# A hybrid layer on one core: the weight sums of a group one slot apart and moved by three or four slots, and each sum stored by itself

## The chip, the cores and the metric

One core of a Trainium2 chip. Its engines are TensorE (PE, matmuls), VectorE (DVE), ScalarE (ACT), GpSimd (POOL) and SyncE (SP). DMA transfers are issued from SP and from ACT. The metric is the device time of one execution in microseconds (us); a kernel's time is the median of its runs.

## The reference

One layer of a streaming encoder, on 256 frames of width 4096, in fp32. One input projection feeds two groups of heads and a gate; a second projection and a LayerNorm close the layer:

```python
proj = einsum('bsd,dc->bsc', x, w_in)
# fox q|k|v|f, rwkv r|k|v|w_down|a_down, gate z
fox_out = fox_attention(q, k, v, log_sigmoid(f + f_bias))   # 16 heads of 128
rwkv_out = groupnorm(rwkv7_scan(r, decay, k, v, -kk, kk * a)) + bonus   # 32 heads of 64, chunks of 64 frames
h = concat([fox_out, rwkv_out]) * silu(z)
out = einsum('bsc,cd->bsd', h, w_out)
x = layernorm(ALPHA * x + out, ln_gain, ln_bias)
```

## The kernel before

**The input projection.** It is cut into 8 groups (n = 0 to 7) of 4 blocks (b = 0 to 3); a block is 512 columns. The 4096 rows of the weights make 32 k tiles of 128. fp32 operands are split in two: a rounded high part and the rest, so each product takes three matmuls per half of the frames (lines 162, 163 and 164: low frames by high weights and so on; line 164 is the one that needs the low part of the weights). Per pair q of k tiles there is one load of 512 KB from SP's queue (line 266, tile `w`), one cast to the high part on ACT (line 156, tile `w_qh`, 4 buffers) and one subtract for the low part on DVE (line 157, tile `w_ql`, 3 buffers). So w_12 is the pair q = 12, k tiles 24 and 25. In the text, w_12 or w_13 without a block number is that of block 1.

**The slots.** After each k tile the loop over a block calls `slot()`, which advances every piece of side work (a generator) by one `yield`. A group has 4 x 32 = 128 slots. Engines run their instructions in the order in which they were issued here, as far as the scheduler leaves it, so a slot is a place in each engine's queue, not a time. The side work of a steady group is:

- `prepare` with `front`: the decays and keys of a head pair. SP loads `raw` (line 330) and the low-rank weights `upt` (line 470); ACT makes `uph` (475), `tw` (487), `ta` (489), `eL` (496) and `eI` (498), both from `L`, which DVE scans (493); then `am` (501), and DVE `ae` (503) from `eI`; then `k` (541), `sb` (544), `hq` and `hr` (510, 512), `lc` (550), `lt` (551, 552) and `BK` (557).
- `rwkv`: the recurrence over four chunks, with matmuls `rh`, `up` and `sp`, whose results ACT and DVE copy to `R` (706), `UV` (737) and `SV` (748); then `yp`, and its norm (`post`, `hqy`, `hry`).
- `gate`: products `h` and their split `hl` (433 to 437), stored to DRAM as `hd` by SP (330). `fox`: attention, with `nb` loaded by SP (796, 797) and `fo` (826). `unload`: the copy `bk` of a finished block out of PSUM by ACT (1125), its transposes and its way through DRAM.
- `weight_sums` (lines 839 to 869), which the change touches.

**The weight sums.** Two pairs of blocks of the output projection use, for eight pairs q of k tiles, differences of four 128x512 blocks of `w_o`. They are made long before, during the input projection: 16 sets, two in each group. A set is four loads of 256 KB into the tile `ts` (128x4x512, one buffer), four subtracts on DVE (line 864, in place) and the stores to a scratch tensor `td` in DRAM, from which the output projection loads them after 1674 us. Loads and stores are issued from ACT's queue, both by `send`, line 847, in program order. `SETS` (line 55) gives for each of a group's two sets the slot at which its loads begin and how many slots later the subtracts may begin. `until` waits for a slot, `wait(n)` lets n slots go by. Since `ts` has one buffer, the loads of a set wait until the stores of the last one have read it.

**The output projection** follows the last group, then the LayerNorm. The change doesn't touch them.

Of the kernel before, what the change touches and what calls it, by code (L numbers as in the profile page):

```python
# [51 lines left out]
TAIL = 3  # L52
STARTS = (3, 5)
RING = (4, 3)
SETS = ((0, 12), (30, 8))
W = {"fo": 7, "vs": 2, "np": 4, "gp": 5, "tp": 4, "d1": 8, "d2": 12, "xp": 3, "fs": 4, "fp": 5}
NB = D // OB

# [37 lines left out]
def layer(ctx: ExitStack, tc: tile.TileContext, xt, xtok, w_main, w_lora, w_first, muv, w_o, up, par, mulora, fbias, lng, lnb, cst, out):  # L96
# [76 lines left out]
    for n, (k0, k1) in enumerate(pieces):  # L173
        for k in range(k0, k1):
            t = xpool.tile([P, 2, S], F32R, tag=f"x{k}", name=f"x{k}")
# [33 lines left out]
    def wait(n):  # L209
        for _ in range(n):  # L210
            yield
# [25 lines left out]
    tds = {(b, q): dram.tile([P, 4, OB], F32, name=f"td{b}_{q}") for b in STARTS for q in FEW}  # L237
# [607 lines left out]
    def weight_sums():  # L845
        def send(out, src):
            tc.keep_in_program_order(nc.scalar.dma_start(out=out, in_=src))

        def until(at):
            while where[0] < at:  # L850
                yield

        per = KT * 4
        places = [(n * per + (0 if n else KT) + o, gap) for n in range(G // 2) for o, gap in SETS]
        for (b, q), (at, gap) in zip(tds, places, strict=True):
            yield from until(at)
            t = rp.tile([P, 4, OB], F32, tag="ts", name=f"ts{b}_{q}")
            for n in range(4):
                send(t[:, n], w_o[b + n // 2][:, 2 * q + n % 2, :])
                yield  # L860
            yield from until(at + gap)
            b11, b21, b12, b22 = (t[:, n] for n in range(4))
            for o, x, y in ((b11, b12, b11), (b12, b22, b12), (b22, b22, b11), (b21, b21, b22)):
                nc.vector.tensor_tensor(o, x, y, ALU.subtract)
                yield from wait(2)
            yield from wait(3)
            for n in (2, 0):
                send(tds[b, q][:, n : n + 2], t[:, n : n + 2])
                yield from wait(2)

    def chain():
        for n in range(G // 2):
# [236 lines left out]
    side(gates())  # L1109
    side(chain())  # L1110
    side(weight_sums())
    vt = None
    for n in range(G // 2):
# [84 lines left out]
    for kind, b, q in plan:  # L1198
# [3 lines left out]
        if pair:  # L1202
            n = count[pair] = count[pair] + 1
# [245 lines left out]
```

## Time and profile before

| | |
|---|---|
| runs | 1912.09 us median of 3 (1911.28 to 1915.17) |
| profiled execution | 1909.98 us, of which the span 1908.2 |
| PE busy | 1897.1 us, 99% |
| DVE busy | 1477.3 us, 77% |
| ACT busy | 1010.5 us, 53% |
| POOL busy | 248.9 us, 13% |
| DMA | 466.75 MB, mean 245 GB/s |
| TensorE clock granted | 0.999 |

The span is the time of the core's work; the execution's own time has 1.8 us around it. In the rows of a timeline the columns are the start in us, the duration in us, the engine, the line, the operation, the output and the inputs; in brackets stands the idle time of the engine just before, and what ended it. "ACTq" and "SPq" are the queues from which DMAs are issued. In a row of the waits, the numbers are the total in us, the number of waits and the longest. In a row of the windows each engine has its busy time and, in brackets, its instructions, in the order PE, weight load, DVE, ACT, POOL; then come the granted clock, the DMA engines' share and GB/s.

### The profile page before, as it was taken

To read this page: it belongs to the slowest core of one execution; us is meant where nothing else is said; L and a number is where in the kernel's file an instruction comes from. 1 tells how busy PE (TensorE), PEld (TensorE's weight loads), DVE (VectorE), ACT (ScalarE), POOL (GpSimd) and SP (SyncE) were. 2 spreads that over 40 slices of the span, in tenths; PEclk is the share of its full clock that TensorE was granted. 3 is DMA by queue.
4 is the path that set the end of the run, shared out by engine and by line. 5 is a ranking of instruction groups with operands and counts; after the bars stand their busy time and mean duration, and the time that the engine had idled before them with its cause. 6 is when DMAs were issued, how large, how long until landed. Compare 5 with 4: busy or idle time off the path is not lost.

```text
span 1908.2 us, 28381 instructions
## 1 busy us (share of the span) xinstructions
PE 1897.1 (99%) x9745; PEld 1573.9 (82%) x9745; DVE 1477.3 (77%) x2521; ACT 1010.5 (53%) x1575; POOL 248.9 (13%) x467
## 2 busy tenths in 40 slices
PE   9999999999999999999999999999999999999998
PEld 9887888888888888888888888888888878888885
DVE  7688878787778777868787887687878775887876
ACT  6554455455545554555456544654465554455552
POOL 0022002211121122112111220122012200000000
PEclk9999999999999999999999999999999999999999
DMA  9688778887788787878787788778877975878883
GB/s 348 204 259 246 220 238 258 234 236 224 249 243 241 225 256 230 247 220 259 227 246 225 252 236 246 221 249 234 249 222 245 299 264 181 275 257 300 301 289 128
DMA packets 288262, 466.75 MB, mean 245 GB/s; under 512 B 144435, under 2 KB 171717, under 8 KB 288117
## 3 DMA queue, kind: packets, MB, share of 16 engines
q1 hardware_dynamic: 274004, 431.03, 73.7%
q10 hardware_dynamic: 14112, 33.90, 4.7%
q8 instruction: 76, 1.25, 0.3%
q14 instruction: 70, 0.57, 0.1%
HBM read 418.43 MB, written 46.42 MB: 244 GB/s over the span
## 4 chain that ended last, share of the span: by engine, by line
PE 96%; DVE 2%; DMA 1%; ACT 1%; issue 0%; SPq 0%; DVEq 0%; ACTq 0%
PE acc L162 24%; PE acc L164 24%; PE acc L163 23%; PE oacc L991 5%; PE oacc L992 5%; PE oacc L994 5%; PE gp L589 1%; PE rh L703 1%; PE p L991 1%; PE p L994 1%; PE p L992 1%; PE up L734 1%; PE sp L744 1%; PE accl L162 1%; PE accl L164 1%; PE accl L163 1%
## 5 line engine op out<-in xcount | busy, mean ns | idle before, releaser
L818 POOL COPY pT<-lg 32x96 f32<-32x96 f32 x128 | 55.3, 432 | 632.3 <-DVE lg L814 627.5
L626 POOL COPY BKt<-BK 32x192 f32<-32x192 f32 x128 | 73.6, 575 | 62.2 <-DVE BK L623 57.2
L659 DVE TENSOR_REDUCE xc<-prod 128x8 f32<-128x16 f32 (+30 forms) x248 | 72.7, 293 | 6.6
L656 DVE TENSOR_TENSOR prod<-Nb,xc 128x8 f32<-128x8 f32 (+30 forms) x248 | 72.3, 291 | 3.0
L157 DVE TENSOR_TENSOR w_0l<-w,w_0h 128x1024 fp32r<-128x1024 f32 x31 | 38.4, 1239 | 34.8 <-ACT w_0h L156 28.9
L157 DVE TENSOR_TENSOR w_15l<-w,w_15h 128x1024 fp32r<-128x1024 f32 x31 | 38.1, 1228 | 26.3 <-issue 17.9
L156 ACT CAST w_0h<-w 128x1024 fp32r<-128x1024 f32 x31 | 32.6, 1052 | 46.8 <-DMA w<-in_w_main_dram 35.1
L799 POOL TENSOR_SCALAR_AFFINE_SELECT nb<-nb 128x128 f32<-128x128 f32 x32 | 17.9, 568 | 301.8 <-DMA nb<-ncd 200.8
L156 ACT CAST w_6h<-w 128x1024 fp32r<-128x1024 f32 x31 | 32.7, 1055 | 43.3 <-PE acc L163 34.1
L157 DVE TENSOR_TENSOR w_2l<-w,w_2h 128x1024 fp32r<-128x1024 f32 x31 | 38.1, 1231 | 21.3 <-PE acc L164 12.5
L156 ACT CAST w_8h<-w 128x1024 fp32r<-128x1024 f32 x31 | 32.6, 1052 | 38.3 <-PE acc L163 18.1
L157 DVE TENSOR_TENSOR w_11l<-w,w_11h 128x1024 fp32r<-128x1024 f32 x31 | 37.9, 1223 | 17.4 <-PE acc L164 8.7
L156 ACT CAST w_10h<-w 128x1024 fp32r<-128x1024 f32 x31 | 32.6, 1053 | 35.2 <-DMA w<-in_w_main_dram 21.7
L157 DVE TENSOR_TENSOR w_6l<-w,w_6h 128x1024 fp32r<-128x1024 f32 x31 | 43.0, 1388 | 10.6 <-PE acc L164 6.8
L156 ACT CAST w_15h<-w 128x1024 fp32r<-128x1024 f32 x31 | 32.6, 1053 | 33.8 <-DMA w<-in_w_main_dram 20.3
L162 PE MATMUL acc<-w_15h,x 128*128 128x512 f32 x124 | 50.2, 405 | 0.0
L162 PE MATMUL acc<-w_9h,x 128*128 128x512 f32 x124 | 50.0, 403 | 0.0
L156 ACT CAST w_14h<-w 128x1024 fp32r<-128x1024 f32 x31 | 32.6, 1052 | 32.7 <-DMA w<-in_w_main_dram 13.5
L162 PE MATMUL acc<-w_14h,x 128*128 128x512 f32 x124 | 49.5, 399 | 0.0
L157 DVE TENSOR_TENSOR w_9l<-w,w_9h 128x1024 fp32r<-128x1024 f32 x31 | 38.0, 1224 | 14.8 <-ACT w_9h L156 9.5
L157 DVE TENSOR_TENSOR w_7l<-w,w_7h 128x1024 fp32r<-128x1024 f32 x31 | 37.9, 1221 | 14.7 <-PE acc L164 8.6
L162 PE MATMUL acc<-w_2h,x 128*128 128x512 f32 x124 | 49.2, 397 | 0.0
(1052 smaller groups left out, 6764.2 us busy)
## 6 DMA issues: line engine op xcount, KB each, us to landing
w<-in_w_main_dram SPq DMA_DIRECT2D x496, 512.0 KB
wo<-in_w_o_dram SPq DMA_DIRECT2D x96, 512.0 KB
ts<-in_w_o_dram ACTq DMA_DIRECT2D x64, 256.0 KB
td<-ts ACTq DMA_DIRECT2D x32, 512.0 KB
e<-td SPq DMA_DIRECT2D x32, 512.0 KB
bt<-bk SPq DMA_DIRECT2D x88, 128.0 KB
Nb<-nd SPq DMA_DIRECT2D x16, 512.0 KB
e<-in_w_o_dram SPq DMA_DIRECT2D x16, 512.0 KB
```

Source lines behind the costliest of these rows:

```text
L156: latest[1] = nc.scalar.copy(hi[:, :n], src[:, :n])
L157: latest[0] = nc.vector.tensor_tensor(lo[:, :n], src[:, :n], hi[:, :n].bitcast(F32), ALU.subtract)
L162: nc.tensor.matmul(acc[:, :n], xs[k][:, 0, tt], hi[:, o : o + n], start=(k == 0), stop=False)
L163: nc.tensor.matmul(acc[:, :n], xs[k][:, 1, tt], hi[:, o : o + n], start=False, stop=False)
L164: nc.tensor.matmul(acc[:, :n], xs[k][:, 0, tt], lo[:, o : o + n], start=False, stop=(k == KT - 1))
L626: nc.gpsimd.tensor_copy(BKt[B * b : B * (b + 1), :, :, B * a : B * (a + 1)], BK[B * a : B * (a + 1), :, : NCH - 1, B * b : B * (b + 1)])
L656: first = nc.vector.tensor_tensor(prod[:, :, :, s + 1 :], nb[:, :, s : s + 1, s + 1 :].to_broadcast([P, 2, NJ, w]), xc[:, :, :, s + 1 :], ...
L659: solved = nc.vector.tensor_reduce(xc[:, :, :, s : s + 1], prod[:, :, :, s:], AX.X, ALU.add)
L818: (nc.gpsimd.tensor_copy if b % 2 else nc.scalar.copy)(pT[B * b : B * (b + 1), :, B * a : B * (a + 1)], lg[B * a : B * (a + 1), :, B * b : ...
L991: nc.tensor.matmul(acc, h, hi, start=n[0] == n[1], stop=False)
L992: nc.tensor.matmul(acc, l, hi, start=False, stop=False)
L994: nc.tensor.matmul(acc, h, lo, start=False, stop=not n[0])
```

## The change

Three things change in `weight_sums` and its table. The sums of a set stand one slot apart and not two. Set 1 of each group keeps its loads (slots 0 to 3) and its sums go from slots 12, 14, 16, 18 to 16, 17, 18, 19; set 2 has its loads one slot earlier (29 to 32) and its sums at 37 to 40 rather than 38, 40, 42, 44. And each of the four results is stored by itself, 256 KB in a DMA, seven slots behind its sum: set 1 at slots 23 to 26, set 2 at 44 to 47. Before, there were two stores of 512 KB, at 23 and 25, and at 49 and 51. Slots up to 31 are in the group's block 0; slot 32 + k is k tile k of block 1.

```diff
-SETS = ((0, 12), (30, 8))
+SETS = ((0, 16), (29, 8))
...
             for o, x, y in ((b11, b12, b11), (b12, b22, b12), (b22, b22, b11), (b21, b21, b22)):
                 nc.vector.tensor_tensor(o, x, y, ALU.subtract)
-                yield from wait(2)
+                yield
             yield from wait(3)
-            for n in (2, 0):
-                send(tds[b, q][:, n : n + 2], t[:, n : n + 2])
-                yield from wait(2)
+            for n in (0, 2, 3, 1):
+                send(tds[b, q][:, n], t[:, n])
+                yield
```

ACT's order in block 1 of group 3, from the cast of w_11 on; `td<-ts` is a store of the sums. Before:

```order
L847 DMA td_11_847<-ts_11_6368 128x1024
L156 CAST w_1_11h<-w_1_11_6643 128x1024
L501 ACTIVATE am_6724<-ta_6695,hka 128x256
L543 ACTIVATE sb_6734<-s_6_6599,prm 128x256
L847 DMA td_11_847<-ts_11_6368 128x1024
L496 ACTIVATE eL_6713<-L_6711 128x4x64
L498 ACTIVATE eI_6716<-L_6711 128x256
L156 CAST w_1_12h<-w_1_12_6668 128x1024
L550 COPY lc_6728<-eL_6713 128x4
L156 CAST w_1_13h<-w_1_13_6698 128x1024
```

The same place after:

```order
L156 CAST w_1_11h<-w_1_11_6659 128x1024
L501 ACTIVATE am_6741<-ta_6713,hka 128x256
L543 ACTIVATE sb_6751<-s_6_6614,prm 128x256
L156 CAST w_1_12h<-w_1_12_6686 128x1024
L156 CAST w_1_13h<-w_1_13_6715 128x1024
L496 ACTIVATE eL_6730<-L_6728 128x4x64
L498 ACTIVATE eI_6733<-L_6728 128x256
L550 COPY lc_6745<-eL_6730 128x4
```

Both stores are gone from there, and eL and eI have moved from ahead of the cast of w_12 to behind the cast of w_13.

ACT's order a little earlier in the same block after the change, at the casts of w_8 to w_10, where no store stood before:

```order
L156 CAST w_1_8h<-w_1_8_6569 128x1024
L847 DMA td_11_847<-ts_11_6350 128x512 x2
L324 ACTIVATE s_6_6611<-raw_6567,omm 128x256
L324 ACTIVATE s_6_6614<-raw_6567,omm 128x256
L436 CAST hl_6629<-h_6627 128x256
L156 CAST w_1_9h<-w_1_9_6598 128x1024
L847 DMA td_11_847<-ts_11_6350 128x512
L475 CAST uph_6679<-upt_5038 96x256
L847 DMA td_11_847<-ts_11_6350 128x512
L156 CAST w_1_10h<-w_1_10_6632 128x1024
```

The four stores of set 2 stand there now, two behind the cast of w_8 and two around uph.

DVE's order in block 1 of group 3, between the scan of L and the split of w_13. Before:

```order
L541 TENSOR_TENSOR k_6732<-s_6_6599,am_6724 128x256
L544 SCALAR_TENSOR_TENSOR sb_6734<-s_6_6596,prm,k_6732 128x256
L503 SCALAR_TENSOR_TENSOR ae_6726<-ta_6695,eI_6716 128x256
L157 TENSOR_TENSOR w_1_12l<-w_1_12_6668,w_1_12h 128x1024
L510 STREAM_TRANSPOSE hq_6750<-sb_6734 128x512
L551 SCALAR_TENSOR_TENSOR lt_6730<-s_6_6599,nkk,eL_6713 128x4x64
L512 TENSOR_REDUCE hr_6752<-hq_6750 128x16
L552 TENSOR_TENSOR lt_6730<-s_6_6596,eL_6713 128x4x64
L157 TENSOR_TENSOR w_1_13l<-w_1_13_6698,w_1_13h 128x1024
```

The same place after:

```order
L541 TENSOR_TENSOR k_6749<-s_6_6614,am_6741 128x256
L157 TENSOR_TENSOR w_1_12l<-w_1_12_6686,w_1_12h 128x1024
L544 SCALAR_TENSOR_TENSOR sb_6751<-s_6_6611,prm,k_6749 128x256
L503 SCALAR_TENSOR_TENSOR ae_6743<-ta_6713,eI_6733 128x256
L510 STREAM_TRANSPOSE hq_6766<-sb_6751 128x512
L551 SCALAR_TENSOR_TENSOR lt_6747<-s_6_6614,nkk,eL_6730 128x4x64
L512 TENSOR_REDUCE hr_6768<-hq_6766 128x16
L552 TENSOR_TENSOR lt_6747<-s_6_6611,eL_6730 128x4x64
L157 TENSOR_TENSOR w_1_13l<-w_1_13_6715,w_1_13h 128x1024
```

The split of w_12 has moved up past sb and ae, and ae, which reads eI, now stands between it and the split of w_13.

## The prediction

> **What bounds the kernel now.** I read the page's head and its chain, then TensorE's waits, then two groups in the table of windows.
>
> ```profile
> span 1908.2 us, 28381 instructions
> PE 1897.1 (99%) x9745; PEld 1573.9 (82%) x9745; DVE 1477.3 (77%) x2521; ACT 1010.5 (53%) x1575; POOL 248.9 (13%) x467
> PE 96%; DVE 2%; DMA 1%; ACT 1%; issue 0%; SPq 0%; DVEq 0%; ACTq 0%
> PE acc L164 <- DVE w_12l L157: 0.9, 1, 0.9
> PE sp L744 <- DVE UV L737: 0.3, 1, 0.3
> PE up L734 <- ACT R L706: 0.3, 1, 0.3
> 588.00:778.00 190.00, 190.00 (x1003) 157.77 (x1002) 148.03 (x267) 101.55 (x165) 29.94 (x56) 1.00 0.80 239
> ```
>
> TensorE (PE) is busy 99% of the span, and 190.00 of 190.00 us in group 3 (588 to 778), at granted clock 1.00. The waits listed between the program's two ends come to 0.9 + 0.3 + 0.3 = 1.5 us. Two things follow. No order of the side work can gain more than about 1.5 us, which is under 0.2% (3.8 us), the least that a measurement of this kernel can tell from no change. And any microsecond for which TensorE is made to wait is lost for good, since nothing later has room to win it back. So the question is whether a weight tile is late anywhere. I looked for the place in a group where weights come closest to late. It is block 1, k tiles 24 to 27 (w_12, w_13), at 672 to 680 us in group 3. ACT first, then DVE, then PE's first use of w_13l:
>
> ```profile
> 672.79 0.42 ACT L496 ACTIVATE eL<-L 128x256 f32<-128x256 f32 x1 [1.31 <-DVE L L493]
> 673.11 0.40 ACT L498 ACTIVATE eI<-L 128x256 f32<-128x256 f32 x1
> 673.42 1.04 ACT L156 CAST w_12h<-w 128x1024 fp32r<-128x1024 f32 x1
> 674.74 1.05 ACT L156 CAST w_13h<-w 128x1024 fp32r<-128x1024 f32 x1 [0.19 <-DMA w<-in_w_main_dram]
> 673.54 0.43 DVE L503 SCALAR_TENSOR_TENSOR ae<-ta,eI 128x256 f32<-128x256 f32 x1
> 674.49 1.23 DVE L157 TENSOR_TENSOR w_12l<-w,w_12h 128x1024 fp32r<-128x1024 f32 x1 [0.52 <-ACT w_12h L156]
> 675.63 0.70 DVE L510 STREAM_TRANSPOSE hq<-sb 128x512 f32<-128x512 f32 x1
> 677.55 1.22 DVE L157 TENSOR_TENSOR w_13l<-w,w_13h 128x1024 fp32r<-128x1024 f32 x1
> 679.15 0.61 PE L164 MATMUL acc<-w_13l,x 128*128 128x512 f32 x2
> ```
>
> w_13l ends at 677.55 + 1.22 = 678.77 and is used at 679.15: 0.38 us to spare. Its cast began on the landing of its load (0.19 us of waiting for DMA, at 674.74), 4.41 us ahead of the use.
>
> **The change part by part. The sums.** There are as many as before:
>
> ```profile
> L864 DVE TENSOR_TENSOR ts<-ts x64: 627/684/1773, 88.0 to 1421.3; 128x512 f32<-128x512 f32 x64
> 614.27 0.29 DVE L737 COPY UV<-up 64x128 f32<-64x128 f32 x1 [0.33 <-ACT UV L737]
> 615.40 1.23 DVE L157 TENSOR_TENSOR w_11l<-w,w_11h 128x1024 fp32r<-128x1024 f32 x1 [0.83 <-PE acc L164]
> 618.65 1.23 DVE L157 TENSOR_TENSOR w_12l<-w,w_12h 128x1024 fp32r<-128x1024 f32 x1 [0.78 <-issue]
> 647.63 0.71 DVE L510 STREAM_TRANSPOSE hqy<-post 128x512 f32<-128x512 f32 x1 [1.46 <-ACT post L771]
> 652.58 1.23 DVE L157 TENSOR_TENSOR w_6l<-w,w_6h 128x1024 fp32r<-128x1024 f32 x1 [0.68 <-PE acc L164]
> 662.15 0.69 DVE L864 TENSOR_TENSOR ts<-ts 128x512 f32<-128x512 f32 x1
> ```
>
> Set 1's sums crowd into slots 16 to 19, about 613 to 618 us in group 3. At most two more of 0.68 us stand there, 1.36 us, against 0.33 + 0.83 + 0.78 = 1.94 us of DVE idle in the same stretch; where a split waits for PE to give its buffer back, a sum ahead of it costs nothing. Were that cover gone, the 0.68 us would fall on the UV copy that PE's up and sp wait for, at most that per group. Set 2's sums go to slots 37 to 40: one into the 1.46 us ahead of hqy, one into the 0.68 us ahead of w_6l; the one at 662.15 goes away from the tight place's run-up, so SP's issues behind DVE's work can come up to 0.69 us earlier. I cost the sums at nothing. They also could remove some of the 1.5 us of waits: I take -0.5 us.
>
> **The stores' issues.** 32 more DMAs on ACT's queue, 0.33 us each (row 668.01, below), run beside ACT's compute rows, at an engine 53% busy: nothing.
>
> **The order around w_13.** The fences on the change show that eL and eI, which stood ahead of w_12h on ACT, now stand behind w_13h; and ae, which needs eI, with the four steps behind it, now stands between w_12l and w_13l. So w_13l now waits for a chain that starts only when w_13 has landed: cast 1.05, eL 0.32 (672.79 to 673.11), eI 0.40, ae 0.43, hq to the start of w_13l 1.92 (675.63 to 677.55), w_13l 1.22. That is 5.34 us, and some 5.2 with the 0.1 us by which neighbours overlap. There were 4.41 us in group 3. In group 4:
>
> ```profile
> 864.22 1.04 ACT L156 CAST w_13h<-w 128x1024 fp32r<-128x1024 f32 x1
> 868.92 0.62 PE L164 MATMUL acc<-w_13l,x 128*128 128x512 f32 x2
> ```
>
> It is 4.70 us there, with no wait for DMA. So with its load landing as before, w_13l is late by 0.8 us in group 3 and by up to 0.5 in the others, where the load may have landed before its cast began; the lower bound there is nothing. I take 0.5 us as the mean.
>
> **The stores' bytes.** The stores of set 2 also move, across SP's queue of loads. Two rows of ACT beside which they are issued now, SP's and ACT's issues of before, and what each queue moved (q1 is SP's, q10 ACT's) in 660 to 666, 666 to 672.5 and 672.5 to 680:
>
> ```profile
> 659.93 1.05 ACT L156 CAST w_8h<-w 128x1024 fp32r<-128x1024 f32 x1
> 662.94 0.41 ACT L475 CAST uph<-upt 96x256 fp32r<-96x256 f32 x1
> 660.88 0.43 SPq L266 DMA_DIRECT2D w<-in_w_main_dram  x1
> 664.79 0.37 SPq L330 DMA_DIRECT2D raw<-bt  x1
> 666.20 1.42 SPq L266 DMA_DIRECT2D w<-in_w_main_dram  x3
> 668.01 0.33 ACTq L847 DMA_DIRECT2D td<-ts  x1
> 669.67 0.33 ACTq L847 DMA_DIRECT2D td<-ts  x1
> q1 hardware_dynamic: 588, 1.58, 83.2%
> ...
> q1 hardware_dynamic: 777, 1.60, 91.6%
> ...
> q1 hardware_dynamic: 701, 1.70, 65.7%
> q10 hardware_dynamic: 288, 1.05, 34.2%
> ```
>
> Before, both stores were issued behind the three loads at 666.20 (w_12 to w_14), and between 666 and 672.5 ACT's queue moved nothing; its 1.05 MB came only after 672.5 and took 34.2% of 7.5 us, 2.57 us of all sixteen DMA engines. Now two of the four stores stand behind w_8h and two beside uph, by ACT's rows at about 660 to 663.5, ahead of raw and of the three loads. The idle DMA time there is 16.8% of 6 us = 1.0 us; in the next 6.5 us some 8%, 0.5 us. The first leaves 2.57 - 1.0 = 1.6 us of delay for w_12 and w_13, both leave 1.07. The lower bound is nothing: set 1's stores show none, and SP's issues may come 0.69 us earlier. I take 0.9 us, near the 1.07 and a little under it for the earlier issue.
>
> The Trainium skill, "DMA: Bandwidth & Descriptors", section "Queues, rings and completion order", says that each DMA engine goes round-robin between the queues that have work. By that rule the two stores would have shared with w_12 and w_13 already before, and moving them up would cost no delay; the 6.5 us in which ACT's queue stood with two stores and moved nothing speak against it here.
>
> **The sum.** w_13l late by 0.5 + 0.9 = 1.4 us per group, in groups 2 to 7 in full (8.4 us), in group 1 half (0.7), less 0.5: +8.6 us. Against the profiled execution's own 1909.98 us that is 1918.6. The runs' median of 1912.09 lies 2.1 above that execution, so I forecast 1920.7 us as the median. With the upper bounds, 0.8 + 1.6 = 2.4 us per group, it is 6.5 x 2.4 - 0.5 = +15.1, and 1927.2.
>
> **The rivals. No change:** w_13 lands in time; in group 3 this is decided at 679.15 - 5.2 = 673.95, against 674.74 before. For it: the stores no longer stand among w_14 and w_15, the DVE is freed of 0.69 us ahead of 666, and the order of w_12l ahead of ae gives w_12l room. If the load lands 1 us sooner than I think, the 1.4 us becomes at most 0.4, and the whole -0.5 to +2.6 us: 1911.6 to 1914.7. Against it: the DMA engines have 1.5 us of idle time for 2.57 us of stores. The round-robin order of the queues leads here as well: no delay by the stores, and lateness only from the order, at 0 to 0.4 us.
>
> **Slower by another way:** ACT stands at the first load into ts, now at slot 29, until the last store of set 1 has landed, since ts has one buffer.
>
> ```profile
> 634.53 0.34 ACTq L847 DMA_DIRECT2D ts<-in_w_o_dram  x1
> 638.44 0.59 ACT L1125 COPY bk<-acc 128x512 f32<-128x512 f32 x1 [0.64 <-PE acc L164]
> ```
>
> Behind it on ACT are w_1h, the exponentials, the bk copies that free PSUM, w_2h and R. Before, that load ran at 634.53; the last store is now issued three slots earlier, about 631 to 632. The stores' 0.26 MB and the loads queued by then make 1 to 5 us of landing. From about 638 on PE would be held, by about 1 us in seven groups: 1919.1. For it stands only that the load is a slot earlier and the last store a slot later.
>
> **Faster:** all 1.5 us of waits vanish and nothing is late: 1910.6. This is still within 0.2%; more could come only from scatter.
>
> **How the numbers follow.** w_13l late by 0.6 us per group or more: 0.58, likeliest. No change: 0.25. ACT at slot 29: 0.10. Faster, small: 0.07, of which 0.04 for beyond 0.2% by scatter. Slower by over 0.2% takes the first and the third: 0.68; within 0.2%: 0.28; faster: 0.04. The range reaches from 1911.0 (no change at its fast end) to 1928.0 (both bounds at their upper ends).
>
> **What would show it.** Right: in groups 2 to 7 PE waits 0.6 to 2.4 us for w_13l of block 1, with DVE's split of it directly behind L552, ACT's eL directly behind w_13h's cast, and w_13h's cast waiting for DMA and starting less than 5.2 us ahead of the time at which PE would have come to w_13l; ACT's queue moves its 1.05 MB ahead of the three loads. Each of these groups takes about 1.4 us longer. Wrong: no wait of PE there; a cast of w_13h over 5.2 us ahead of w_13l's use; ACT's queue idle between 660 and 672 though the stores have been issued; or PE waiting at slots 29 to 33.

## The result, and the profile after

The changed kernel takes 1923.33 us, the median of 4 runs (1922.33 to 1924.95), against 1912.01 us before: a ratio of 1.0057, 95% interval 1.0039 to 1.0074. The forecast was 1920.7, slower. The profiled execution took 1923.88 us, 13.9 more than that of before. The page's head and its chain by engine:

```profile
span 1922.1 us, 28428 instructions
PE 1903.3 (99%) x9745; PEld 1572.7 (82%) x9745; DVE 1484.2 (77%) x2521; ACT 1008.6 (52%) x1575; POOL 257.2 (13%) x467
PE 83%; DVE 8%; DMA 5%; ACT 2%; issue 2%; SPq 0%; POOL 0%; ACTq 0%; DVEq 0%; POOLq 0%
```

PE's share of the chain that ended last fell from 96% to 83%. That doesn't mean that PE stood for 17% of the time, for it is busy 99%: from each wait the chain is followed back along the engine that was waited for, and it now leaves PE more often. The waits of PE say for what (total, times, longest):

```profile
PE acc L162 <- ACT w_11h L156: 3.2, 5, 1.4
PE acc L164 <- DVE w_13l L157: 3.0, 7, 0.6
PE acc L164 <- DVE w_12l L157: 1.1, 1, 1.1
```

The third was there before, with 0.9. The wait for w_13l, 7 times, is the one forecast. The wait for w_11h was not forecast. These two add up to 6.2 us only, since the ends of matmuls are modelled, a part of each stop is counted as busy, and short stops aren't listed. The whole price shows in the length of block 1. The first matmul of blocks 1 and 2 of group 3, before:

```profile
638.24 0.40 PE L162 MATMUL acc<-w_0h,x 128*128 128x512 f32 x1
...
686.40 0.39 PE L162 MATMUL acc<-w_0h,x 128*128 128x512 f32 x1
```

The same two after:

```profile
642.70 0.39 PE L162 MATMUL acc<-w_0h,x 128*128 128x512 f32 x1
...
693.63 0.39 PE L162 MATMUL acc<-w_0h,x 128*128 128x512 f32 x1
```

That is 48.16 us before and 50.93 after: 2.77 us lost in one block. Read the same way, block 1 grew by 1.52, 2.05, 2.76, 1.86, 1.36, 1.63 and 1.22 us in groups 1 to 7, 12.4 of the 13.9 us. By the starts of the matmuls, 4.2 us of it were lost ahead of the first matmul with w_11h, 3.3 more within the pair w_11, where its low part came late, 0.9 within w_12 and 4.6 within w_13; the rest of the block gained 0.6. Here is where it was lost in group 3. PE:

```profile
677.01 0.39 PE L164 MATMUL acc<-w_10l,x 128*128 128x512 f32 x1
678.79 0.50 PE L162 MATMUL acc<-w_11h,x 128*128 128x512 f32 x1 [1.39 <-ACT w_11h L156]
...
685.49 0.39 PE L163 MATMUL acc<-w_13h,x 128*128 128x512 f32 x1
686.25 0.74 PE L164 MATMUL acc<-w_13l,x 128*128 128x512 f32 x2 [0.37 <-DVE w_13l L157]
```

ACT and its queue in the same stretch, and SP's issue of raw:

```profile
664.86 0.33 ACTq L847 DMA_DIRECT2D td<-ts  x1
667.06 1.27 ACTq L847 DMA_DIRECT2D td<-ts  x1
668.21 0.37 SPq L330 DMA_DIRECT2D raw<-bt  x1
676.53 0.91 ACT L324 ACTIVATE s<-raw,omm 128x256 f32<-128x256 f32 x2 [2.97 <-DMA raw<-bt]
677.71 1.03 ACT L156 CAST w_11h<-w 128x1024 fp32r<-128x1024 f32 x1
680.48 1.05 ACT L156 CAST w_13h<-w 128x1024 fp32r<-128x1024 f32 x1
681.43 0.41 ACT L496 ACTIVATE eL<-L 128x256 f32<-128x256 f32 x1
681.75 0.41 ACT L498 ACTIVATE eI<-L 128x256 f32<-128x256 f32 x1
```

The same uses of raw, cast of w_11 and split of w_11 before:

```profile
668.37 0.90 ACT L324 ACTIVATE s<-raw,omm 128x256 f32<-128x256 f32 x2
669.53 1.04 ACT L156 CAST w_11h<-w 128x1024 fp32r<-128x1024 f32 x1
670.60 1.22 DVE L157 TENSOR_TENSOR w_11l<-w,w_11h 128x1024 fp32r<-128x1024 f32 x1 [0.81 <-ACT w_11h L156]
```

And three rows of DVE after:

```profile
678.77 1.23 DVE L157 TENSOR_TENSOR w_11l<-w,w_11h 128x1024 fp32r<-128x1024 f32 x1 [0.81 <-DMA w<-in_w_main_dram]
682.72 0.41 DVE L503 SCALAR_TENSOR_TENSOR ae<-ta,eI 128x256 f32<-128x256 f32 x1
684.98 1.21 DVE L157 TENSOR_TENSOR w_13l<-w,w_13h 128x1024 fp32r<-128x1024 f32 x1
```

Read the ACT rows from the top. The stores are issued from 664.86 on, and the last one just ahead of raw. raw, issued at 668.21, lets ACT go on only at 676.53, 8.3 us later; before, it was issued at 664.79 and its use ran at 668.37, which had not waited for it. ACT stands idle for 2.97 us ahead of `s`, its first use of raw, and the cast of w_11, next but one in ACT's queue, waits with it. PE wanted w_11h at 677.01 + 0.23 = 677.24 and got it at 678.79. Below, eL and eI stand behind the cast of w_13, as the order showed, and w_13l is late by 0.76 - 0.23 = 0.53 us. But eI isn't what held it. eI ended at 681.75 + 0.41 = 682.16, and DVE came to ae only at 682.72. From the split of w_11 to that of w_13 DVE's instructions follow one another with no idle time listed. That run starts 36.07 us after the block's first matmul, against 32.36 before, because the split of w_11 needs its cast. So the late cast of w_11 reached PE twice: at w_11, and by way of DVE at w_13l.

### The profile page after: what moved, and what is told of

It reads as the page before. It is cut to its first block, busy times and chain, and to the rows that moved or that the text cites. A ratio compares the mean times of both kernels' runs of the same rounds, so it can differ in the third digit from the quotient of the medians.

```text
span 1922.1 us, 28428 instructions
## 1 busy us (share of the span) xinstructions
PE 1903.3 (99%) x9745; PEld 1572.7 (82%) x9745; DVE 1484.2 (77%) x2521; ACT 1008.6 (52%) x1575; POOL 257.2 (13%) x467
## 4 chain that ended last, share of the span: by engine, by line
PE 83%; DVE 8%; DMA 5%; ACT 2%; issue 2%; SPq 0%; POOL 0%; ACTq 0%; DVEq 0%; POOLq 0%
PE acc L164 20%; PE acc L162 20%; PE acc L163 19%; PE oacc L991 5%; PE oacc L994 5%; PE oacc L992 5%; DMA raw<-bt 2%; DMA w<-in_w_main_dram 2%; PE gp L589 1%; PE rh L703 1%; PE p L991 1%; PE p L994 1%; PE p L992 1%; PE up L734 1%; DVE w_11l L157 1%
## 5 line engine op out<-in xcount | busy, mean ns | idle before, releaser
L162 PE MATMUL acc<-w_11h,x 128*128 128x512 f32 x124 | 49.8, 402 | 3.2 <-ACT w_11h L156 3.2
L164 PE MATMUL acc<-w_13l,x 128*128 128x512 f32 x124 | 48.5, 400 | 3.0 <-DVE w_13l L157 3.0
L156 ACT CAST w_1h<-w 128x1024 fp32r<-128x1024 f32 x31 | 32.6, 1052 | 35.9 <-DMA w<-in_w_main_dram 23.2
L157 DVE TENSOR_TENSOR w_10l<-w,w_10h 128x1024 fp32r<-128x1024 f32 x31 | 37.9, 1223 | 16.7 <-ACT w_10h L156 7.3
L156 ACT CAST w_9h<-w 128x1024 fp32r<-128x1024 f32 x31 | 32.6, 1051 | 34.0 <-DMA w<-in_w_main_dram 21.2
L164 PE MATMUL acc<-w_12l,x 128*128 128x512 f32 x124 | 49.2, 397 | 1.1 <-DVE w_12l L157 1.1
```

Source lines behind the costliest of these rows:

```text
L156: latest[1] = nc.scalar.copy(hi[:, :n], src[:, :n])
L157: latest[0] = nc.vector.tensor_tensor(lo[:, :n], src[:, :n], hi[:, :n].bitcast(F32), ALU.subtract)
L162: nc.tensor.matmul(acc[:, :n], xs[k][:, 0, tt], hi[:, o : o + n], start=(k == 0), stop=False)
L164: nc.tensor.matmul(acc[:, :n], xs[k][:, 0, tt], lo[:, o : o + n], start=False, stop=(k == KT - 1))
```

## The experiments

Four theories. **In-order:** set 2's early stores hold raw back, and ACT, working in order, carries that on to the cast of w_11, which is behind raw's first use. **Sums:** the new places of the sums and loads cost by themselves. **Split:** four DMAs in place of two are what costs. **Order term:** eL and eI behind the cast of w_13 cost 0.3 to 0.8 us per group. All ratios are against the kernel before on the same chip.

**late_stores.** Set 2's stores alone go back:

```diff
-            yield from wait(3)
+            yield from wait(8 if gap == 8 else 3)
```

> The changed kernel with the stores of set 2 alone put back, at slots 49 to 52 (still four of 256 KB). If the loss comes from the bytes of these stores standing ahead of raw and the weights (bytes theory), the waits of PE for w_11h and w_13l of block 1 go, and the time is 1911 to 1914 us. If it comes from the new places of the sums (sums theory), it stays at 1920 to 1924. If it comes from the halved stores (split theory), at least half stays: 1917 or more.

1915.03 us, 1.0018 (1.0009 to 1.0028). 7.5 of the 11.3 us are gone, and so are the waits for w_11h and w_13l, but it stays slower than before by 0.2%, a little above what was expected. Its own rows show another loss. ACT, at the same place of group 3:

```profile
677.37 0.33 ACTq L847 DMA_DIRECT2D td<-ts  x1
677.74 0.20 ACT L550 COPY lc<-eL 128x4 f32<-128x4 f32 x1 [1.88 <-DMA td<-ts]
677.84 1.04 ACT L156 CAST w_13h<-w 128x1024 fp32r<-128x1024 f32 x1
```

ACT stood still for 1.88 us until a store had landed, between two issues of stores, and the cast of w_13 behind it too. In group 3 this costs nothing: block 1 is as long as before. In groups 4 to 6 the same stop is 3.0 to 3.2 us long and block 1 grows by 0.8 to 1.1 us; PE waits twice for w_13h, 1.0 us in all. It also waits 2.1 us for w_5l and 1.0 for R; where these come from was not followed further. So the early stores were the larger part.

**early_stores.** The kernel before, with set 2's two whole stores moved up:

```diff
                 nc.vector.tensor_tensor(o, x, y, ALU.subtract)
-                yield from wait(2)
-            yield from wait(3)
+                yield from wait(1 if gap == 8 else 2)
+            yield from wait(2 if gap == 8 else 3)
```

> The kernel before with the two stores of 512 KB of set 2 alone moved up, to slots 44 and 46 (for that its four sums stand one slot apart, from slot 38). Bytes theory: 1918 to 1923 us, raw lands over 3 us later against its block than before; on ACT the cast of w_11 stands ahead of the use of raw here, so that PE's wait moves from w_11h to w_12 or w_13. Sums theory and split theory: 1911 to 1914.

1914.84 us, 1.0019 (1.0009 to 1.0028): slower, but by 3.6 us and not by 6 to 11. Early stores alone are not the whole loss; it matters what stands behind raw. Here the cast of w_11 stands ahead of it, and PE has no listed wait for w_11h. Instead that cast waits for its own load, as ACT shows in group 3:

```profile
667.92 1.05 ACT L156 CAST w_11h<-w 128x1024 fp32r<-128x1024 f32 x1 [2.70 <-DMA w<-in_w_main_dram]
```

Whether raw lands over 3 us later can't be seen: its uses run right behind the cast of w_11, with no wait for DMA.

**split_only** and **sums_only**, the other two parts of the change by themselves on the kernel before:

```diff
-            for n in (2, 0):
-                send(tds[b, q][:, n : n + 2], t[:, n : n + 2])
-                yield from wait(2)
+            for n in (0, 2, 3, 1):
+                send(tds[b, q][:, n], t[:, n])
+                yield
```

> The kernel before with each set stored in four parts of 256 KB, from slots 23 and 49 on, one slot apart; sums where they were. Bytes theory and sums theory: 1911 to 1914 us. Split theory: 1916 to 1923, and more DMA time on ACT's queue per byte.

1912.14 us, 1.0001 (0.9992 to 1.0011).

```diff
-SETS = ((0, 12), (30, 8))
+SETS = ((0, 16), (29, 8))
...
                 nc.vector.tensor_tensor(o, x, y, ALU.subtract)
-                yield from wait(2)
-            yield from wait(3)
+                yield
+            yield from wait(8 if gap == 8 else 3)
```

> The kernel before with the new places of the loads and sums alone; two stores of 512 KB where they were, at slots 23 and 25, 49 and 51. Bytes theory and split theory: 1911 to 1914 us. Sums theory: 1918 to 1924, with PE waiting for R, UV or w_13l.

1911.69 us, 1.0003 (0.9994 to 1.0013). Neither the split nor the sums cost anything alone that the times show. late_stores has both together and costs 3.8 us.

**early_split.** As early_stores, with the four stores of split_only, from slot 44.

> The kernel before with set 2's sums one slot apart from slot 38 and its stores as four of 256 KB at slots 44 to 47; everything of set 1 but the splitting of its stores, and the loads of set 2, where they were. On ACT the uses of raw (L324) stand ahead of the cast of w_11, as in the changed kernel. In-order theory (the stores hold raw back by some 3 us, and the casts behind its uses on ACT wait with it): 1919 to 1924 us, ACT waiting for raw 1 to 3 us per group. Split theory (four DMAs in place of two are what costs): 1919 to 1924 too. Sums theory (the new places of sums and loads add the rest): 1913 to 1916.

1918.4 us, 1.0035 (1.0022 to 1.0048): 7 us slower, 4.3 short of the loss of the whole change and just below the range expected. PE has six waits for w_13l (2.0 us) and none for w_11h. What ACT waited for raw in all groups, from the view of the tile raw:

```profile
  DMA raw<-bt: 7.0, 7
```

In the changed kernel the same line reads:

```profile
  DMA raw<-bt: 14.0, 7
```

With 1 us of waiting per group, w_11h just comes in time (in three groups w_11l is late by 0.25 to 0.5 us); with 2 it does not.

**early_whole.** The changed kernel with two stores per set (the lines of split_only taken back).

> The changed kernel with two stores of 512 KB per set in place of four of 256 KB, from the same slots, 44 and 46. The cast of w_11 stands ahead of the uses of raw on ACT here. In-order theory and split theory: 1911 to 1916 us, no wait of PE for w_11h. Sums theory: 1919 to 1924.

1914.76 us, 1.002 (1.0011 to 1.003). No wait for w_11h, as the cast of w_11 stands ahead of raw's use here. But the edit changed two things, the split and that order, so it doesn't tell them apart. The next one does.

**cast_first.** The changed kernel with all its stores and sums; only the uses of the group's second raw are moved, behind the cast of w_11:

```diff
-                yield from wait(LAND)
+                yield from wait(LAND + 5 * u)
```

> The changed kernel with the uses of the second raw of a group five slots later, so that they stand behind the cast of w_11 on ACT (eL and eI then stand ahead of the cast of w_13 again); stores as in the changed kernel, split and early. In-order theory: PE's waits for w_11h and w_13l go, 1911 to 1916 us, though raw lands as late as in the changed kernel. Split theory: 1919 to 1924.

1911.18 us, 0.9997 (0.9988 to 1.0006). By the median the whole loss is gone, with the early, split stores still there. ACT in group 3:

```profile
670.14 1.05 ACT L156 CAST w_11h<-w 128x1024 fp32r<-128x1024 f32 x1
672.44 0.91 ACT L324 ACTIVATE s<-raw,omm 128x256 f32<-128x256 f32 x2 [1.26 <-DMA raw<-bt]
674.52 1.05 ACT L156 CAST w_12h<-w 128x1024 fp32r<-128x1024 f32 x1 [0.27 <-DMA w<-in_w_main_dram]
```

raw is waited for here too, until 672.44, 33.4 us after the block's first matmul (676.53 - 642.70 = 33.8 in the changed kernel). But no cast that PE needs soon stands behind it. What comes late from raw can still cost: in groups 2 and 3 of the profile block 1 is 0.7 and 0.9 us longer than before, at w_13. The edit also puts eL and eI ahead of the cast of w_13 again, so it undoes both orders at once; that the second of them cost next to nothing is read from the rows of the changed kernel (DVE reached ae after eI was ready), not from this run.

**half_early.** The changed kernel with two of set 2's four stores early and two late:

```diff
-                yield
+                yield from wait(6 if gap == 8 and n == 2 else 1)
```

> The changed kernel with only two of set 2's four stores early (slots 44 and 45), the other two at slots 51 and 52. On ACT the uses of raw stand ahead of the cast of w_11 as in the changed kernel; eL and eI ahead of the cast of w_13. In-order theory: with half the bytes ahead of raw, ACT's wait for raw (1.4 to 3 us per group in the changed kernel) goes or falls under 1 us, PE's waits for w_11h go: 1911 to 1915 us. If early stores in any amount, or the splitting, are what costs: 1918 or more.

1910.62 us, 0.9996 (0.9987 to 1.0005). The cast of w_11 is behind raw's use, as in the changed kernel; with half the bytes ahead of it, ACT's wait for raw falls from 14.0 us in 7 waits to 1.8 in 2, and the loss is gone. So early stores as such don't cost; the amount does. (As in cast_first, eL and eI stand ahead of the cast of w_13 here.)

**stores_gap.** The kernel before with set 2's sums at slots 37 to 40 and its two stores at 41 and 42, into the stretch in which the DMA engines stood idle:

```diff
-SETS = ((0, 12), (30, 8))
+SETS = ((0, 12), (29, 8))
...
-                yield from wait(2)
-            yield from wait(3)
+                yield from wait(1 if gap == 8 else 2)
+            yield from wait(0 if gap == 8 else 3)
             for n in (2, 0):
...
-                yield from wait(2)
+                yield from wait(1 if gap == 8 else 2)
```

> The kernel before with set 2's loads at slots 29 to 32, its sums at 37 to 40 and its two stores of 512 KB at slots 41 and 42, ahead of the stretch of a group in which the DMA engines are idle (0.16 of 655 to 660 us before). If the place of the bytes decides, nothing is lost and the waits at w_12 to w_14 may go: 1909 to 1913 us. If any early store costs, 1914 or more.

1909.3 us, 0.9989 (0.998 to 0.9999): faster than both kernels, by 2.1 us against before (interval 0.2 to 3.8 us). The waits listed before don't explain it, for most of them are still there: 0.9 us for w_12l and 0.4 for UV. In the profile block 1 is 0.6 us shorter in group 1 and 0.2 in group 2; where the rest comes from stays open. The queues in 651 to 659 us of it:

```profile
q1 hardware_dynamic: 574, 1.21, 40.5%
q10 hardware_dynamic: 288, 1.05, 32.0%
```

All of the set's 1.05 MB moved ahead of the loads that follow.

**gap_and_before_raw.** stores_gap with its second store one slot later, at 43 and not at 44 as the expectation says (the last `wait(1 if gap == 8 else 2)` is `wait(2)` again). It is issued 23.4 us after the block's first matmul, ahead of raw. ACT and DVE then have the changed kernel's order around w_13.

> The kernel with set 2's stores in the gap (1909.3 us) with its second store two slots later, at 44, so that 0.5 MB stands ahead of raw again; on ACT and DVE the orders from the cast of w_11 to the split of w_13 are those of the changed kernel (eL and eI behind the cast of w_13). Order term of the prediction (w_13l late by 0.3 to 0.8 us per group by the order alone): PE waits for w_13l in most groups and w_11h in none, 1912 to 1916 us. If the order alone costs nothing: 1909 to 1911.

1913.21 us, 1.0013 (1.0003 to 1.0022). PE in group 3:

```profile
678.54 0.39 PE L163 MATMUL acc<-w_13h,x 128*128 128x512 f32 x1
679.00 0.74 PE L164 MATMUL acc<-w_13l,x 128*128 128x512 f32 x2
```

From the one to the other stand 0.46 us where a matmul takes 0.23; the first two of w_13l are slow as well. Block 1 is 0.36 to 0.40 us longer than before in groups 3 to 7, all of it at k tiles 26 and 27; w_11 is in time. In group 2, where ACT waits 0.8 us for raw, it is 1.0 us longer. The time falls into the range of the order theory, but the rows don't show its mechanism. ACT and DVE in group 3:

```profile
668.95 0.47 ACT L487 ACTIVATE tw<-lp,half 128x256 f32<-128x256 f32 x1 [2.76 <-PE lp L485]
671.56 1.23 DVE L157 TENSOR_TENSOR w_11l<-w,w_11h 128x1024 fp32r<-128x1024 f32 x1 [0.82 <-ACT w_11h L156]
674.54 0.40 ACT L498 ACTIVATE eI<-L 128x256 f32<-128x256 f32 x1
675.48 0.41 DVE L503 SCALAR_TENSOR_TENSOR ae<-ta,eI 128x256 f32<-128x256 f32 x1
```

eI was ready at 674.94, 0.54 us before DVE came to ae, and DVE has no listed idle time from the split of w_11 to that of w_13. What is later is again the start of that run: 33.70 us after the block's first matmul (671.56 - 637.86), against 32.36 before. The cast of w_11 stands on ACT behind tw, tw waits for PE's product lp, and PE runs the last matmul of lp 1.3 us later in its order (30.78 us into the block, 29.44 before). So w_13l is late here by about 0.4 us per group, and the place of eL and eI isn't the cause.

**set2_later** and **set1_before** ask for the 4 us between early_split and the changed kernel. They differ from early_split by one edit each.

```diff
-SETS = ((0, 16), (29, 8))
+SETS = ((0, 16), (30, 8))
...
-            yield from wait(3)
+            yield from wait(2 if gap == 8 else 3)
```

> The changed kernel with set 2's loads and sums one slot later (loads 30 to 33, sums 38 to 41), its stores still from slot 44. It stands between the changed kernel (1923.3 us) and the kernel with early split stores alone (1918.4). If the remaining 4 to 5 us between those two come from set 2's earlier loads and sums, 1917 to 1920, and ACT waits for raw by about 1 us as there; if from set 1's new places, 1922 to 1925.

1921.77 us, 1.0055 (1.004 to 1.007).

```diff
-SETS = ((0, 16), (29, 8))
+SETS = ((0, 12), (29, 8))
...
-                yield
+                yield from wait(1 if gap == 8 else 2)
```

> The changed kernel with set 1's sums where they were before, at slots 12, 14, 16 and 18; its split stores and all of set 2 as changed. If the remaining 4 to 5 us come from set 1's new places, 1917 to 1920; if from set 2's earlier loads and sums, 1922 to 1925.

1925.82 us, 1.0072 (1.0056 to 1.0089). Both times lie outside the ranges expected. Against before on their own chips they are 9.2 and 13.2 us slower, where early_split is 7.0 and the changed kernel 11.3. So each of the two edits alone brings back some of the rest, they don't add up, and the runs don't decide between the two. What follows the time is ACT's wait for raw, in all groups: 7.0 us in early_split (1918.4 us), 12.3 in set2_later (1921.8), 14.0 in the changed kernel (1923.3), 14.9 in set1_before (1925.8). Block 1 of groups 1 to 7 grew by 5.9, 10.8, 12.4 and 13.7 us in these four profiles. In group 3, SP issues raw 24.96, 25.53, 25.51 and 26.01 us after the block's first matmul in these four (SP's row less PE's). So the sums do act, once the early stores are there, with raw issued later by 0.5 to 1 us. Which instruction passes that on was not tried.

## Why the prediction was right

**What bounds the kernel:** right. PE is at 99%, and what it waited for was lost for good: block 1 grew, and nothing later gave it back.

**The sums cost nothing:** right alone (sums_only 1.0003). Together with the early stores they cost: 2.2 us (set2_later less early_split, each against before on its chip) and 6.3 (set1_before less early_split), and ACT's wait for raw grows with them. The prediction did not see that.

**The order around w_13:** right in place, near in size, wrong in mechanism. Forecast were 0.5 us per group without the stores, and gap_and_before_raw shows 0.4. But the chain that was priced, from the cast of w_13 over eL and eI to ae, held DVE in a single group: only in group 4 of the changed kernel did it stand for eI, 0.2 us. The prediction's own signs say so. The cast of w_13 was to wait for its load and to start less than 5.2 us ahead of PE. No group lists a wait of it for its load, and in group 3 it starts 685.72 - 680.48 = 5.24 us ahead, in six of groups 1 to 7 it is 5.2 us or more. What set w_13l is DVE's run of 6.2 us from the split of w_11 to that of w_13, which begins when the cast of w_11 is done. The sum has no such term. That 0.5 came near 0.4 is luck.

**The stores' bytes:** the mechanism was right, and the step that followed it to its end failed. The prediction said that the stores stand "ahead of raw and of the three loads", and then charged the delay to w_12 and w_13 alone, 0.9 us. raw itself, named in the same sentence, was never followed to its user. Its use is on ACT ahead of the cast of w_11, and raw came 33.8 us after the block's start against 30.1 at the latest before: at least 3.7 us later, not 0.9 to 1.6. The margin of w_11 was not priced at all. In group 3, 1.55 us of the 2.77 were lost where PE waited for w_11h, and some 0.5 more at w_11l. The loads of w_12 and w_13, to which the 0.9 us was charged, held their casts up once in seven groups (w_12, 0.5 us in group 4); what more they were late can't show behind the late cast of w_11. Nor did the stores use the idle time that the prediction gave them: issued from 664.86 on, they had moved 0.02 MB by 668.

**The sum:** 1.4 us per group were forecast for groups 2 to 7, and they lost 1.2 to 2.8, mean 1.8; group 1 lost 1.5, not 0.7. The total of +8.6 was +11.3 between the medians. It came near because two errors met: w_13l was late by less than the 1.4 (0.65 to 0.88 us in groups 2 to 7, read as the growth of its pair of k tiles) and by another way, and w_11, not priced, made up for it. So that stores ahead of raw make the kernel slower was foreseen; that the number fits is luck.

**The rivals.** ACT at slot 29: not seen; block 0 takes 50.14 us in groups 4 and 5 against 50.24 and 50.25 before. No change: it came true with w_11's cast ahead of raw's use (cast_first) and with half the bytes (half_early). In cast_first a move of raw's uses on ACT was enough.

**The round-robin rule.** The Trainium skill ("DMA: Bandwidth & Descriptors", section "Queues, rings and completion order") says that each DMA engine takes turns between the queues that have work. The prediction held 666 to 672.5 us of before against it, but the first of the two stores was issued only at 668.01, so they stood 4.5 us at most and not 6.5. The run after shows both queues at work at once, in 668 to 674:

```profile
q1 hardware_dynamic: 681, 1.39, 60.3%
q10 hardware_dynamic: 561, 1.02, 44.2%
```

With stores and loads moving side by side there, this agrees with the rule, and the earlier stretch shows only that a store's bytes can start late: in the changed kernel, with the issues from 664.86 on, only 0.02 MB had moved by 668; before, with the issue at 668.01, none had by 672.5. Sharing did not spare raw, though: the stores took 44% of the engines just when raw was due.

## What to carry to other kernels

When a transfer is moved ahead of others in a queue, list every transfer that it now precedes, and for each one follow the engine that waits for it, in order, to the first thing behind that the bound engine needs. A tile with no hurry of its own can hold up the next cast if it is used just ahead of it on an engine that takes its instructions in order, as ACT does here. A late cast then shows twice, at its own use and wherever another engine's work lines up behind it. And before a wait is put down to a new order, look whether the engine really stood for the instruction named: here eI was ready half a microsecond before DVE came to it. Three cures were seen here: an order (the use moved behind the cast), a gap (the bytes sent while the DMA engines stand idle) and half the bytes.

## What the runs showed of the hardware

Storing the same bytes in parts of 256 KB took more of the DMA engines. The page of before has 14112 packets, 33.90 MB and 4.7% of 1908.2 us on ACT's queue; after:

```profile
q10 hardware_dynamic: 18720, 33.91, 5.0%
```

By these rounded shares that is some 96 us of all sixteen engines in place of 90, about 0.4 us more per set. split_only has the same 5.0% and shows that it costs no time by itself.

A stop of PE costs more than the idle time that this profile gives it. In the changed kernel's group 3 the profile gives PE an idle time of 1.39 us at w_11h, while the starts around it lie 1.78 us apart, 1.55 more than the 0.23 between matmuls. Over the kernel, the 6.2 us of waits for w_11h and w_13l stand beside 12.4 us of growth, of which the 3.3 at w_11l are in no listed wait.
